# A four-byte tile gets a 64-byte slot, and every tile laid out after it moves by 32 bytes

## The chip, the core and the metric

The kernel is one program on one core of a Trainium2 chip. The metric is the device time of one execution in microseconds. Three executions of the kernel before gave a median of 2630.83 us (2629.59 to 2634.77).

## What is computed

Sixteen sublayers in a row work on one sequence of 256 tokens with 1024 features, all in float32. Cut to what matters here:

```python
# f00 f01 f10 f11: gated feed-forward, width 2816;  g00 g01 g10 g11: the same, width 2752, modulated
h = (silu(gate) * up) @ w_out            # gate, up = x @ w_in
# m0 m1: squared relu, width 4096
h = square(relu(u @ w_ff1)) @ w_ff2
# conv, hgrn (recurrent mixer), dsa, diff, pool, moba: mixers, each ending in
m = o @ w_out                            # o: 256 x 1024, w_out: 1024 x 1024
# pool and moba also attend to a memory
k, v = split(mem_n @ w_mem_kv)
```

Every sublayer is wrapped in an RMS norm and added to `x`.

## The kernel before

The order of the sublayers is f00, conv, f01, f10, hgrn, f11, g00, dsa, g01, g10, diff, g11, pool, m0, moba, m1.

**Weights.** All large weights lie in `wall` as 413 chunks of 1 MB, in the order in which they are used. `_load` (L314) brings a chunk into a `raw` tile (3 buffers). `_split` (L321) makes two float32r tiles of it: ScalarE copies four pieces into `hi` (L330), VectorE subtracts and writes the rest into `lo` (L335); each has 5 buffers. An activation is split the same way into a high and a low tile, and a product is three matmuls: high with high, high with low, low with high.

**Matmuls.** In each, one operand is loaded into the array as a block of 128 x 128 (the profile's PEld, LDWEIGHTS) and the other streams past it (PE, MATMUL). In the profile's `out<-in` the streaming tile is named first and the loaded one second, and the shape behind is that of the streaming operand. Four places matter:

- `u_products` (L545, matmuls at L552 to L554): blocks of `hi` or `lo` are loaded, `xh` or `xl` streams with 256 columns.
- `proj_pair` (L574, L581 to L583): blocks of `xh` or `xl` are loaded, `hi` or `lo` streams with 512 columns. Each sublayer's first products are of this kind, and so is `mem_kv` (L1598), whose loaded tiles are `mh` and `ml`.
- `downs` (L612, L622): a block of the hidden tile is loaded, and `hi` or `lo` streams with 512 columns. In the ten feed-forward blocks the hidden tiles are `hh` and `hl`; in the mixers' output products they are `xh` and `xl`, except in hgrn, where they are `ov` and `oscT` (L1084).
- transposes (L503, L526, L760, L1252, L1331): the tile is loaded, `ident` streams.

The lines of `downs` that pick the operands:

```python
mm = lambda l, r, i, st, sp: nc.tensor.matmul(
    acc[i], lhsT=l[:k, t], rhs=r[:k, 1024 * b + 512 * i:1024 * b + 512 * i + 512], ...)
    yield mm(hh, wh, i, ...)
    yield mm(hh, wl, i, ...)
    yield mm(hl, wh, i, ...)
```

**Where tiles lie.** Pools are stacked in the order in which they are opened (L300 to L307):

```python
self.cst = pool("cst", 1)
self.raw_p = pool("rawp", self.RB)
self.hi_p = pool("hip", self.HB)
self.lo_p = pool("lop", self.HB)
self.act = pool("act", 1)
self.rowp = pool("rowp", 1)
self.tmp = pool("tmp", 1)
self.tiny = pool("tiny", 4)
```

Each sublayer opens its own pools on top of these and closes them at its end. A slot is a whole number of 32-byte steps of each partition. In the built program `hi` begins at byte 54496, 62688, ... of a partition, `lo` at 95456, ..., `xh` at 136416 and `xl` at 144608: all of them 224 bytes past a multiple of 512. The slot of the tile `prime` in `tiny` lies at 172640, and the sublayers' pools begin at 174784, which is 192 past a multiple of 512. `hh` lies at 180928, 182976, ..., `hl` at 189120, ... (207552 and more in m0 and m1), `oscT` at 174784, `ov` at 187072, `mh` at 178880 and `ml` at 187072: all of them at 192.

**The tile that is changed.** `prime` (L432) runs a one-element activation whose result nobody reads, so that ScalarE has the next function's table before it is needed. `finish` (L638) calls it at a sublayer's end, and `conv` once.

Of the kernel before, what the change touches and what calls it, by code (L numbers as in the profile page):

```python
# [11 lines left out]
F32 = mybir.dt.float32  # L12
# [280 lines left out]
class _K:  # L293
# [138 lines left out]
    def prime(self, func, after):  # L432

        n = after.shape[0]
        t = self.tiny.tile([128, 1], F32, name="prime", bufs=1)
        self.nc.scalar.activation(t[:n], after, func, scale=0.0)

    def square(self, src, st, n):
# [1396 lines left out]
```

## Time and profile before

| | |
|---|---|
| median of three executions | 2630.83 us |
| the profiled execution | 2628.67 us |
| its span, from the first to the last instruction | 2626.9 us |
| mean granted TensorE clock | 0.997 |
| HBM read | 550.62 MB, 210 GB/s over the span |

The span is 1.8 us shorter than the time of the same execution. Times inside a profile are microseconds from the span's start. In the profile f00 ends at about 203 us, conv at 336, f01 at 526, f10 at 716, hgrn at 872, f11 at 1063, g00 at 1251, dsa at 1358, g01 at 1546, g10 at 1734, diff at 1856, g11 at 2056, pool at 2125, m0 at 2323, moba at 2440.

### The profile page before, as it was taken

What the parts mean: (1) busy time and instruction counts of PE and PEld (TensorE: products, weight loads), DVE (VectorE), ACT (ScalarE), POOL (GpSimd) and SP (SyncE); (2) the same over time, 40 slices, a digit from 0 to 9 for tenths busy, and PEclk for the clock granted to TensorE, in tenths of its full rate; (3) what the DMA queues carried; (4) which work ended last, traced back from release to release, by engine and by line L of the source; (5) the groups of instructions that cost most, each with busy time, mean ns of one, the idle gap of its engine ahead of it and who ended that gap; (6) DMA issues with size and microseconds to landing.
All of it is one profiled execution on the core that took longest, in us unless ns stands there. A gap on an engine that the chain in (4) does not pass through costs nothing.

```text
span 2626.9 us, 43032 instructions
## 1 busy us (share of the span) xinstructions
PE 2585.0 (98%) x15958; PEld 2286.7 (87%) x15958; DVE 1914.4 (73%) x5151; ACT 1374.9 (52%) x3037; POOL 71.6 (3%) x158
## 2 busy tenths in 40 slices
PE   8999999999999999999999999999999999999999
PEld 7998889989998899899779989977899788977898
DVE  7858587587578875985878778677855866577754
ACT  5545454454545544644664454466644655466543
POOL 0000000000000000000000000000100000000000
PEclk9999999999999999999999999999999999999999
DMA  8847376486425675784548768653555545542552
GB/s 325 305 161 281 145 259 246 150 331 233 169 92 194 258 288 177 279 307 175 177 162 303 264 230 332 219 210 129 210 191 177 187 162 197 187 170 97 192 182 91
DMA packets 92739, 554.53 MB, mean 211 GB/s; under 512 B 10717, under 2 KB 11757, under 8 KB 38385
## 3 DMA queue, kind: packets, MB, share of 16 engines
q1 hardware_dynamic: 92528, 551.79, 57.4%
q8 instruction: 125, 2.05, 0.3%
q14 instruction: 86, 0.70, 0.1%
HBM read 550.62 MB, written 1.13 MB: 210 GB/s over the span
## 4 chain that ended last, share of the span: by engine, by line
PE 58%; issue 34%; DVE 3%; ACT 2%; POOL 1%; DMA 1%; SPq 0%; POOLq 0%; ACTq 0%; DVEq 0%
PE a L622 20%; PE ps L552 8%; PE ps L553 8%; PE ps L554 8%; PE a L581 2%; PE a L583 2%; PE a L582 2%; DVE lo L335 2%; PE a L903 1%; PE tr L503 1%; DMA raw<-in_wall 1%; POOL ry L447 1%; ACT hi L330 1%; ACT junk L441 1%; PE a L1303 0%
## 5 line engine op out<-in xcount | busy, mean ns | idle before, releaser
L335 DVE TENSOR_TENSOR lo<-raw,hi 128x256 fp32r<-128x256 f32 (+1 forms) x2964 | 1158.1, 448 | 387.3 <-ACT hi L330 386.8
L330 ACT ACTIVATE hi<-raw 128x512 fp32r<-128x512 f32 x1652 | 944.3, 623 | 759.2 <-issue 271.3
L552 PE MATMUL ps<-xh,hi 128*128 128x256 f32 x2784 | 789.9, 284 | 0.0
L553 PE MATMUL ps<-xl,hi 128*128 128x256 f32 x2784 | 788.5, 283 | 0.0
L554 PE MATMUL ps<-xh,lo 128*128 128x256 f32 x2784 | 788.2, 283 | 0.0
L553 PEld LDWEIGHTS ps<-xl,hi 128*128 128x128 f32 x2784 | 533.4, 192 | 3.6
L552 PEld LDWEIGHTS ps<-xh,hi 128*128 128x128 f32 x2784 | 533.3, 192 | 3.6
L554 PEld LDWEIGHTS ps<-xh,lo 128*128 128x128 f32 x2784 | 533.4, 192 | 0.1
L622 PE MATMUL a<-hi,hh 128*128 128x512 f32 x960 | 309.6, 396 | 0.0
L622 PE MATMUL a<-lo,hh 128*128 128x512 f32 x960 | 309.3, 396 | 0.0
L622 PE MATMUL a<-hi,hl 128*128 128x512 f32 x960 | 309.3, 396 | 0.0
L622 PEld LDWEIGHTS a<-lo,hh 128*128 128x128 f32 x960 | 179.9, 188 | 43.7
L622 PEld LDWEIGHTS a<-hi,hl 128*128 128x128 f32 x960 | 179.9, 187 | 43.5
L1159 DVE SCALAR_TENSOR_TENSOR adaj<-adaw,cond 128x1024 bf16<-128x1024 f32 x144 | 175.6, 1219 | 42.8 <-DMA adaw<-in_ada 41.6
L622 PEld LDWEIGHTS a<-hi,hh 128*128 128x128 f32 x960 | 174.5, 188 | 36.2 <-ACT hh L697 0.2
L581 PE MATMUL a<-hi,xh 128*128 128x512 f32 x512 | 201.4, 394 | 3.2 <-ACT xh L511 1.8
L583 PE MATMUL a<-hi,xl 128*128 128x512 f32 x512 | 201.9, 396 | 0.6 <-DVE xl L512 0.6
L582 PE MATMUL a<-lo,xh 128*128 128x512 f32 x512 | 200.1, 391 | 0.3 <-DVE lo L335 0.3
L581 PEld LDWEIGHTS a<-hi,xh 128*128 128x128 f32 x512 | 96.6, 189 | 26.5 <-ACT xh L516 5.4
L583 PEld LDWEIGHTS a<-hi,xl 128*128 128x128 f32 x512 | 96.3, 188 | 24.7 <-DVE xl L512 3.2
L582 PEld LDWEIGHTS a<-lo,xh 128*128 128x128 f32 x512 | 96.6, 189 | 20.6 <-DVE lo L335 0.8
L735 ACT ACTIVATE hh<-h 128x256 fp32r<-128x256 f32 x144 | 59.1, 410 | 71.9 <-DVE h L734 71.9
(364 smaller groups left out, 2607.5 us busy)
## 6 DMA issues: line engine op xcount, KB each, us to landing
raw<-in_wall SPq DMA_DIRECT2D x413, 1024.0 KB, 4.8
adaw<-in_ada SPq DMA_DIRECT2D x144, 512.0 KB, 6.8
taps<-in_ctaps SPq DMA_DIRECT2D x10, 1024.0 KB, 7.8
G<-in_rows SPq DMA_DIRECT2D x16, 512.0 KB, 5.7
pg<-in_rows SPq DMA_DIRECT2D x12, 512.0 KB, 4.9
xn<-modd SPq DMA_DIRECT2D x12, 512.0 KB
cond<-condd SPq DMA_DIRECT2D x7, 512.0 KB, 6.1
memt<-in_mem SPq DMA_DIRECT2D x4, 512.0 KB, 3.3
```

What stands on the lines that cost most here:

```text
L330: self.nc.scalar.activation(h[:, c], r[:, c], AF.Copy)
L335: self.nc.vector.tensor_tensor(l[:, c], r[:, c], h[:, c].bitcast(F32), op=OP.subtract)
L441: self.nc.scalar.activation(j, src, AF.Square, scale=1.0 / 32, accum_out=st[:, n:n + 1])
L552: yield self.nc.tensor.matmul(o, lhsT=wh[:, c], rhs=xh[:, k, :], start=(k == 0), stop=False)
L553: yield self.nc.tensor.matmul(o, lhsT=wh[:, c], rhs=xl[:, k, :], start=False, stop=False)
L554: yield self.nc.tensor.matmul(o, lhsT=wl[:, c], rhs=xh[:, k, :], start=False, stop=(k == 7))
L581: yield self.nc.tensor.matmul(p, lhsT=xh[:, k, t], rhs=wh[:, c], start=(k == 0), stop=False)
L582: yield self.nc.tensor.matmul(p, lhsT=xh[:, k, t], rhs=wl[:, c], start=False, stop=False)
L583: yield self.nc.tensor.matmul(p, lhsT=xl[:, k, t], rhs=wh[:, c], start=False, stop=(k == 7))
L622: mm = lambda l, r, i, st, sp: nc.tensor.matmul(acc[i], lhsT=l[:k, t], rhs=r[:k, 1024 * b + 512 * i:1024 * b + 512 * i + 512], start=st, s ...
L735: nc.scalar.activation(hh[:n, b], h[:n], AF.Copy)
L1159: self.nc.vector.scalar_tensor_tensor(junk, self.ada_w.pop(n), 1.0, self.cond, op0=OP.mult, op1=OP.mult, accum_out=self.mods[k][:, c:c + 1])
```

## The change

The tile has 16 elements instead of 1, and its first column is used as before:

```diff
     def prime(self, func, after):
 
         n = after.shape[0]
-        t = self.tiny.tile([128, 1], F32, name="prime", bufs=1)
+
+        t = self.tiny.tile([128, 16], F32, name="prime", bufs=1)[:, :1]
         self.nc.scalar.activation(t[:n], after, func, scale=0.0)
```

Its slot grows from 32 to 64 bytes. The instructions on each engine and their order stay the same. Whatever lies below or before that slot stays: `hi`, `lo`, `xh`, `xl`, `raw`, the rows, `ident`. Whatever comes after it in `tiny`, and every pool of a sublayer, begins 32 bytes later: `hh`, `hl`, `oscT`, `ov`, `mh` and `ml` now lie 224 past a multiple of 512, as the weights do. The mixers' other tiles move by 32 bytes as well, all of one sublayer together.

## Rows read from the trace of the kernel before

**Rows 1.** The page's head and first part: busy time, share, instructions.
```profile
span 2626.9 us, 43032 instructions
...
PE 2585.0 (98%) x15958; PEld 2286.7 (87%) x15958; DVE 1914.4 (73%) x5151; ACT 1374.9 (52%) x3037; POOL 71.6 (3%) x158
```
**Rows 2.** The page's fifth part: output products of the feed-forward blocks (busy us, mean ns).
```profile
L622 PE MATMUL a<-hi,hh 128*128 128x512 f32 x960 | 309.6, 396 | 0.0
L622 PE MATMUL a<-lo,hh 128*128 128x512 f32 x960 | 309.3, 396 | 0.0
L622 PE MATMUL a<-hi,hl 128*128 128x512 f32 x960 | 309.3, 396 | 0.0
```
**Rows 3.** Busy time by engine, most of f01: start:end length, engines, PEclk, DMA share.
```profile
345.00:525.00 180.00, 179.95 (x1205) 165.30 (x1204) 128.38 (x346) 86.68 (x184) 1.72 (x4) 1.00 0.64 228
```
**Rows 4.** Timeline of f01, PE: start us, length us, instruction; 18 rows of two between.
```profile
513.84 0.63 PE L622 MATMUL a<-hi,hh 128*128 128x512 f32 x2
514.31 0.63 PE L622 MATMUL a<-lo,hh 128*128 128x512 f32 x2
...
522.24 0.39 PE L622 MATMUL a<-hi,hh 128*128 128x512 f32 x1
```
**Rows 5.** Timeline of conv's output product, PE; 16 rows of two from first to last.
```profile
315.89 0.62 PE L622 MATMUL a<-hi,xl 128*128 128x512 f32 x2
316.35 0.61 PE L622 MATMUL a<-hi,xh 128*128 128x512 f32 x2
...
323.15 0.39 PE L622 MATMUL a<-hi,xh 128*128 128x512 f32 x1
```
**Rows 6.** Timeline of hgrn's output product, PE; 18 rows of two from first to last.
```profile
860.43 0.63 PE L622 MATMUL a<-hi,ov 128*128 128x512 f32 x2
...
868.83 0.39 PE L622 MATMUL a<-hi,ov 128*128 128x512 f32 x1
```
**Rows 7.** Timeline of moba's memory keys, PE; 25 single matmuls from first to last.
```profile
2316.26 0.40 PE L581 MATMUL ps<-hi,mh 128*128 128x512 f32 x1
...
2322.09 0.39 PE L582 MATMUL ps<-lo,mh 128*128 128x512 f32 x1
```
**Rows 8.** Timeline of the same lines with xh in hgrn; 22 single matmuls.
```profile
842.62 0.39 PE L581 MATMUL ps<-hi,xh 128*128 128x512 f32 x1
...
847.61 0.39 PE L582 MATMUL ps<-lo,xh 128*128 128x512 f32 x1
```
**Rows 9.** Instructions of L622: ns min/median/max of one, first and last start.
```profile
L622 PE MATMUL a<-hi,hh x960: 390/394/497, 48.8 to 2622.3; 128*128 128x512 f32 x192
L622 PE MATMUL a<-lo,hh x960: 392/396/486, 49.2 to 2622.5; 128*128 128x512 f32 x192
...
L622 PE MATMUL a<-hi,xh x160: 387/389/794, 308.6 to 2439.0; 128*128 128x512 f32 x160
...
L622 PE MATMUL a<-hi,ov x32: 393/394/397, 848.1 to 871.8; 128*128 128x512 f32 x32
```
**Rows 10.** VectorE by shape: busy us, mean ns, idle before.
```profile
L335 DVE TENSOR_TENSOR lo<-raw,hi 128x256 fp32r<-128x256 f32 x2624 | 939.4, 417 | 358.1 <-ACT hi L330 357.6
...
L736 DVE TENSOR_TENSOR hl<-h,hh 128x256 fp32r<-128x256 f32 x140 | 58.5, 418 | 1.3 <-ACT hh L735 1.3
```
**Rows 11.** PE by shape, transposes: busy us, mean ns, idle before.
```profile
L503 PE MATMUL tr<-ident,xn 128*128 128x128 f32 x300 | 41.3, 277 | 10.5 <-DVE xn L488 10.4
L1331 PE MATMUL tr<-ident,e 128*128 128x128 f32 x140 | 24.0, 278 | 0.6 <-DVE xl L1277 0.2 <-ACT e L1321 0.2
L1252 PE MATMUL tr<-ident,on 128*128 128x128 f32 x52 | 8.2, 275 | 0.4 <-DVE on L1525 0.4
```
**Rows 12.** Busy time by engine in conv at the lower clock (columns as in Rows 3).
```profile
309.00:314.00 5.00, 5.00 (x13) 3.84 (x13) 3.72 (x8) 4.71 (x10) 0.00 (x0) 0.50 0.00 0
```
**Rows 13.** Timeline of that stretch, PE; four rows of two from first to last.
```profile
309.63 1.05 PE L622 MATMUL a<-lo,xh 128*128 128x512 f32 x2
...
313.05 1.05 PE L622 MATMUL a<-hi,xl 128*128 128x512 f32 x2
```

## The prediction

> **What bounds the kernel now.** I read the page's head first. TensorE's matmuls take 2585.0 of 2626.9 us, VectorE 73% and ScalarE 52% [rows 1], so the question is what sets TensorE's pace. One stage answers it: over 180 us of f01 TensorE is busy for 179.95, VectorE for 128.38 (71%), ScalarE for 86.68 (48%), and the DMA engines for 0.64 of the time [rows 3]. Nothing makes TensorE wait there. A feed-forward block is then as long as its matmuls in a row, and one that starts sooner after its predecessor shortens the block by that much.
>
> The length of a matmul in the profile is not this pace, since matmuls overlap. The pace is the distance between starts, and the timeline gives it. In f01, 18 rows of two matmuls of L622, all on `hh` and `hl`, lie between the starts 513.84 and 522.24: 8.40 us / 36 = 233.3 ns each [rows 4]. In conv's output product, the same line, shape and weights, but with `xh` and `xl` loaded, 16 rows of two lie between 315.89 and 323.15: 7.26 / 32 = 226.9 ns [rows 5]. Both run back to back at the full clock. Why 6.4 ns more?
>
> Three places tell. hgrn's output product loads `ov` and `oscT`, tiles with the shape of `xh` but in a sublayer's own pool: 8.40 / 36 = 233.3 ns [rows 6]. The memory's keys use L581 to L583 with `mh` and `ml`, again of `xh`'s shape: 5.83 / 25 = 233.2 ns [rows 7]. The same lines with `xh` take 4.99 / 22 = 226.8 ns [rows 8]. So neither the line nor the shape nor the way the tile is stepped through sets the pace. What the slow three share is that the loaded tile lies 192 bytes past a multiple of 512 while the streaming `hi` or `lo` lies at 224; in the fast two both lie at 224. The durations say the same: 394 to 396 ns in the median for `hh` and 394 for `ov`, 389 for `xh` [rows 9].
>
> **The change, part by part.** It adds, removes and reorders no instruction. The ten activations that write `prime` still write one element for each partition; their cost is unchanged. What is left is where tiles lie.
>
> *Output products of the feed-forward blocks.* `hh` and `hl` move to 224, so the pair becomes the fast one. There are 3 x 960 = 2880 such matmuls [rows 2] (264 in each of eight blocks, 384 in m0 and m1). 2880 x (233.3 - 226.9) ns = 18.4 us, all of it on the path, since TensorE never pauses there [rows 3].
>
> *hgrn's output.* 96 matmuls on `ov` and `oscT` x 6.4 ns = 0.6 us.
>
> *Memory keys and values*, two sublayers, 96 matmuls on `mh` and `ml`: 96 x (233.2 - 226.8) = 0.6 us. They stand between g11 and pool, and between m0 and moba, back to back with the next products.
>
> *What doesn't change.* The 256-column products stream `xh` past `hi`, neither of which moves. In conv the two float32r tiles that move, `ones` and `bias`, move together, as do the mixers' own float32 pairs.
>
> *Transposes.* Here `ident` stays and the loaded tile moves. The trace has no such tile at its new place, so I bound it by tiles that lie at different places already: `xn` at 224, `e` at 256, 224, 192 and 448, `on` at 256, 224, 192 and 448, which take 277, 278 and 275 ns [rows 11]. A spread of 3 ns over at most some 300 moved transposes is 0.9 us either way; I take zero.
>
> *VectorE and ScalarE* write and read the moved tiles. `lo`, at 224, takes 417 ns for 256 columns, `hl`, at 192, takes 418 [rows 10]: one nanosecond, either way, on engines that are 71% and 48% busy in the block. Zero; the cover is TensorE's own row of matmuls, and without it 144 such instructions would be 0.1 us.
>
> *Sum.* 18.4 + 0.6 + 0.6 = 19.6 us less. The profiled execution took 2628.67 us with a span of 2626.9, so the changed one should take 2609.1 with a span of 2607.3. The median of the three executions lies 2.2 us above the profiled one; **from it I forecast 2611.2 us**.
>
> *Its bounds.* By durations alone [rows 9] a matmul gains 5 to 7 ns: 3072 x 5 = 15 us to 3072 x 7 = 21.5 us. Next late, once the blocks are 1.7 us shorter, is still TensorE: VectorE's 128.38 us in a stretch of 178.3 is 72%.
>
> A rule speaks against all this. The Trainium skill, page "TensorE: Matmul & The Clock Gate", section "Step-by-step: what each phase is for", says that TensorE has two independent read ports into SBUF, one for the streaming operand and one for the weight load, so that loading the next weights takes nothing from the running matmul. By that rule the place of a tile would cost nothing, and the time would stay at 2630.8 us. The trace does not agree with it where the two paces differ for one line and one shape (233.3 against 226.9 ns), though it can't say by itself that the offset is the cause.
>
> **The rivals.**
>
> *No effect.* The pace comes from something else that `hh`, `ov` and `mh` share and `xh` lacks; what remains is that they all lie above byte 174784, `xh` below 152800. A tile that moves by 32 bytes would then gain nothing: 2630.8 us. For it: no row before has a float32r tile in that upper part at offset 224. Against it: within the slow group `hh` and `ov` lie anywhere from 174784 to 211648 and show the same 233.3, and `hi` at 54496 or `lo` at 128224 make no difference either; only the offset in 512 is common to each group. 6%.
>
> *The gain is eaten by the feeding of weights.* The blocks would need 0.9% more bytes in a given time. If chunks then came late half the time, half the gain would stay: 2630.8 - 9.8 = 2621.0 us. For it: the DMA engines are already at 0.64 in f01. Against it: TensorE waits for no weights there, and two chunks stand ready in front of it. 4%.
>
> *Slower, by the clock.* In conv TensorE works at half the clock, 1.2 instead of 2.4 GHz, for a stretch [rows 12]: there the same line takes 3.42 / 8 = 427.5 ns [rows 13], so a stretch of 10 us costs about 5 us. It follows a pause of TensorE in the mixer. If earlier ends of the blocks shifted such pauses so that more of them drew a fall, the loss would have to exceed 19.6 us plus the 5.3 us that 0.2% are: five stretches of 10 us in the six mixers where there is one now. 2630.8 - 19.6 + 5 x 5.1 = 2636.7 us. Against it: the pauses in the mixers are made by their own chains, which the change leaves alone; the mean clock is 0.997. 2%.
>
> **How the numbers follow.** The forecast has 88%. The low end takes the largest gain and the one stretch at half the clock in conv gone, from the fastest of the three executions: 2629.6 - 21.5 - 5 = 2603 us. The high end takes the smallest gain from the slowest of the three: 2634.8 - 15 = 2620 us. This leaves out the rivals (12%) and a little of the forecast's own tails. A measurement can tell about 0.2%, or 5.3 us, from no change. Faster by more: the forecast and the half-eaten gain, 0.92. The same: no effect, 0.06. Slower: 0.02.
>
> **What would show it.** Right: L622 on `hh` and `ov` at a median of about 389 ns, rows of two starting 0.45 instead of 0.47 us apart, `mh` like `xh`; the products of 256 columns, `lo` and the transposes as before; each feed-forward block about 1.7 us shorter, m0 and m1 2.4, the conv, dsa, diff and pool sublayers as long as before; TensorE's busy time near 2565 us. Wrong: `hh` still at 394 to 396 ns (no effect); `hh` at 389 with TensorE waiting for `hi` or `lo` in the blocks (eaten gain); `hh` at 389, the blocks shorter, and the mixers longer at a lower granted clock (slower).

## The result and the profile after

The changed kernel took 2617.28 us in the median of five executions (2615.37 to 2621.91), the kernel before 2633.18 beside it; the ratio is 0.995, with an interval of 0.994 to 0.9961. That is about 16 us faster, where 19.6 were forecast. The profiled execution took 2617.28 us with a span of 2615.5. Code from L435 on stands one line lower in this kernel: L622 is now L623, L581 is L582.

The page's head, part 1 and three groups of part 5 of the kernel after (columns as in [rows 1, 2]):

```profile
span 2615.5 us, 43032 instructions
...
PE 2571.4 (98%) x15958; PEld 2291.9 (88%) x15958; DVE 1913.1 (73%) x5151; ACT 1377.0 (53%) x3037; POOL 69.7 (3%) x158
...
L623 PE MATMUL a<-hi,hh 128*128 128x512 f32 x960 | 305.1, 392 | 0.0
L623 PE MATMUL a<-lo,hh 128*128 128x512 f32 x960 | 304.1, 391 | 0.0
L623 PE MATMUL a<-hi,hl 128*128 128x512 f32 x960 | 303.7, 391 | 0.0
```

TensorE has 13.6 us less of busy time with the same instructions; VectorE and ScalarE are where they were. The durations of L623 show where it is (ns, minimum, median and maximum, as in [rows 9]):

```profile
L623 PE MATMUL a<-hi,hh x960: 388/389/500, 49.7 to 2610.9; 128*128 128x512 f32 x192
L623 PE MATMUL a<-lo,hh x960: 387/389/482, 50.1 to 2611.2; 128*128 128x512 f32 x192
...
L623 PE MATMUL a<-hi,xh x160: 387/390/795, 307.4 to 2429.7; 128*128 128x512 f32 x160
...
L623 PE MATMUL a<-hi,ov x32: 387/389/397, 848.2 to 871.5; 128*128 128x512 f32 x32
```

`hh` and `ov` are at 389 ns, as `xh` already was. The timeline of PE in f01 (start, length) gives the pace of the stretch that [rows 4] showed, between fourteen rows of two:

```profile
512.83 0.61 PE L623 MATMUL a<-lo,hh 128*128 128x512 f32 x2
513.28 0.62 PE L623 MATMUL a<-hi,hl 128*128 128x512 f32 x2
...
519.18 0.39 PE L623 MATMUL a<-hi,hh 128*128 128x512 f32 x1
```

6.35 us / 28 = 226.8 ns from start to start. The memory's keys in the timeline, 33 single matmuls (before: [rows 7]):

```profile
2305.80 0.39 PE L582 MATMUL ps<-hi,mh 128*128 128x512 f32 x1
...
2313.05 0.39 PE L584 MATMUL ps<-hi,ml 128*128 128x512 f32 x1
```

7.25 / 32 = 226.6 ns, against 233.2. TensorE is still what bounds a block; the window of f01 (columns as in [rows 3]):

```profile
345.00:525.00 180.00, 179.91 (x1208) 166.43 (x1207) 129.81 (x348) 87.92 (x187) 2.58 (x6) 1.00 0.64 233
```

**By sublayer.** I cut each trace where a sublayer's first product starts (f00 where its transposes start). The ten feed-forward blocks together take 1901.0 us, 14.5 less than before (1915.5). In this count the memories' keys and values belong to the blocks that they follow, g11 and m0; each of the two went from 11.2 to 10.9 us, so that the blocks' own products gave 13.9 us. The single block f01 went from 190.1 to 188.3, f10 from 190.4 to 189.1, m1 from 187.2 to 185.1. The six mixers together take 706.9, 3.0 more (703.9). Nearly all of that is hgrn, 156.2 to 160.2. Its waits in the kernel after (who waited for whom, us, times, longest):

```profile
DVE masks L1050 <- DMA xn<-in_k_masks: 6.1, 1, 6.1
...
ACT hi L330 <- DVE lo L335: 3.4, 1, 3.4
...
PE tr L690 <- ACT junk L688: 2.8, 1, 2.8
```

In the kernel before, these three were:

```profile
DVE masks L1049 <- DMA xn<-in_k_masks: 3.9, 1, 3.9
...
ACT hi L330 <- DVE lo L335: 1.2, 1, 1.2
...
PE tr L689 <- ACT junk L687: 0.6, 1, 0.6
```

VectorE waited 2.2 us longer for a table of constants, ScalarE stood behind VectorE, and TensorE behind ScalarE. After that pause TensorE worked at half the clock (1.2 GHz) for 3.4 us, as the window shows (columns as in [rows 3]):

```profile
739.90:743.30 3.40, 3.40 (x18) 3.40 (x17) 1.96 (x5) 3.39 (x8) 0.00 (x0) 0.50 0.77 313
```

Is that the change's doing? The first experiment asks it.

### The profile page after: what moved, and what is told of

Its sections match the earlier page's. It is cut to its first block, busy times and chain, and to the rows that moved or that the text cites. A ratio compares the mean times of both kernels' runs of the same rounds, so it can differ in the third digit from the quotient of the medians.

```text
span 2615.5 us, 43032 instructions
## 1 busy us (share of the span) xinstructions
PE 2571.4 (98%) x15958; PEld 2291.9 (88%) x15958; DVE 1913.1 (73%) x5151; ACT 1377.0 (53%) x3037; POOL 69.7 (3%) x158
## 4 chain that ended last, share of the span: by engine, by line
PE 57%; issue 35%; DVE 3%; ACT 2%; POOL 1%; DMA 1%; SPq 0%; POOLq 0%; ACTq 0%; DVEq 0%
PE a L623 19%; PE ps L554 8%; PE ps L555 8%; PE ps L553 8%; PE a L582 2%; PE a L584 2%; PE a L583 2%; PE a L904 1%; DVE lo L335 1%; PE tr L504 1%; ACT hi L330 1%; DMA raw<-in_wall 1%; ACT junk L442 1%; POOL ry L448 1%; PE a L1304 0%
## 5 line engine op out<-in xcount | busy, mean ns | idle before, releaser
L553 PE MATMUL ps<-xh,hi 128*128 128x256 f32 x2784 | 791.1, 284 | 0.0
L554 PE MATMUL ps<-xl,hi 128*128 128x256 f32 x2784 | 790.4, 284 | 0.0
L555 PE MATMUL ps<-xh,lo 128*128 128x256 f32 x2784 | 790.2, 284 | 0.0
L553 PEld LDWEIGHTS ps<-xh,hi 128*128 128x128 f32 x2784 | 535.2, 192 | 3.1
L554 PEld LDWEIGHTS ps<-xl,hi 128*128 128x128 f32 x2784 | 535.2, 192 | 3.0
L555 PEld LDWEIGHTS ps<-xh,lo 128*128 128x128 f32 x2784 | 535.2, 192 | 0.1
L623 PE MATMUL a<-hi,hh 128*128 128x512 f32 x960 | 305.1, 392 | 0.0
L623 PE MATMUL a<-lo,hh 128*128 128x512 f32 x960 | 304.1, 391 | 0.0
L623 PE MATMUL a<-hi,hl 128*128 128x512 f32 x960 | 303.7, 391 | 0.0
L623 PEld LDWEIGHTS a<-lo,hh 128*128 128x128 f32 x960 | 180.3, 188 | 38.1
L623 PEld LDWEIGHTS a<-hi,hl 128*128 128x128 f32 x960 | 180.3, 188 | 37.6
L582 PE MATMUL a<-hi,xh 128*128 128x512 f32 x512 | 202.1, 395 | 3.7 <-ACT xh L512 1.8
L623 PEld LDWEIGHTS a<-hi,hh 128*128 128x128 f32 x960 | 175.2, 189 | 31.3 <-ACT hh L698 0.2
L582 PEld LDWEIGHTS a<-hi,xh 128*128 128x128 f32 x512 | 97.1, 190 | 26.8 <-ACT xh L517 5.4
```

The costliest lines, as they stand in the source:

```text
L553: yield self.nc.tensor.matmul(o, lhsT=wh[:, c], rhs=xh[:, k, :], start=(k == 0), stop=False)
L554: yield self.nc.tensor.matmul(o, lhsT=wh[:, c], rhs=xl[:, k, :], start=False, stop=False)
L555: yield self.nc.tensor.matmul(o, lhsT=wl[:, c], rhs=xh[:, k, :], start=False, stop=(k == 7))
L582: yield self.nc.tensor.matmul(p, lhsT=xh[:, k, t], rhs=wh[:, c], start=(k == 0), stop=False)
L623: mm = lambda l, r, i, st, sp: nc.tensor.matmul(acc[i], lhsT=l[:k, t], rhs=r[:k, 1024 * b + 512 * i:1024 * b + 512 * i + 512], start=st, s ...
```

## The experiments

The ratios are to the kernel before, run beside each. "Pace" is, over all matmuls of a kind in the profiled execution, the mean distance to the start of the next matmul, without gaps (over 150 ns for 256 columns, 260 for 512). For L622 on `hh` and `hl` it went from 233.2 to 227.6 ns with the change.

**The changed kernel again** (no edit).

> The changed kernel once more, to see how much of the missing 4 us is chance. If hgrn's 4 us came from the moved tiles, hgrn takes about 160 us again and its masks land 2 us late again; if from one execution's transfers and clock, hgrn is back near 156 us and the time falls towards 2613 us. L623 on hh keeps a median of 389 ns either way.

2613.94 us (2611.06 to 2615.12), ratio 0.9933 [0.9921, 0.9946]. The profiled execution has a span of 2609.3. Its ten blocks take 1901.0 us, the same as in the first profile of this kernel; its mixers take 700.6 instead of 706.9, with hgrn at 156.1. The same window of hgrn:

```profile
739.90:743.30 3.40, 3.36 (x29) 3.01 (x27) 3.09 (x8) 3.40 (x10) 0.00 (x0) 1.00 0.19 77
```

Full clock, and VectorE waited 3.9 us for the masks, as before. So hgrn's 4 us come and go from one execution to the next. From here on the blocks' sum is my measure of the change, and the whole time only where a ratio has an interval.

**One half of the change each.** Blocks alone: `prime` as before, and in the feed-forward pools

```diff
+            pad = hp.tile([128, 8], F32, name="pad", bufs=1)
+            nc.gpsimd.memset(pad[:, :1], 0.0)
```

> The old prime tile, and a pad of 32 bytes at the bottom of the feed-forward blocks' own pools: hh and hl lie at 224, all mixers' tiles where they were. Theory (the offset sets the pace): hh at 389 ns, ov and mh still at 394 to 396, 16 to 18 us less than before. Rival (the moved mixer tiles took 4 us back): hgrn at 156 us and a time about 3 us below that of the changed kernel.

2617.25 us, ratio 0.9948 [0.9936, 0.9961]; blocks 1902.4. In its profile hgrn takes 160.9 us with every tile of the mixers where it was, so a long hgrn needs no moved tile. The others alone: the changed kernel with the same `pad` of 120 elements, which puts `hh` and `hl` back to 192 in 512:

> The new prime tile, and a pad in the blocks' pools that puts hh and hl back at 192: only ov, oscT, mh, ml and the mixers' other tiles move. Theory: hh at 394 to 396 ns, ov and mh at 389, 1.2 us less than before, which is within what a measurement can tell. Rival (moving the mixers' tiles costs): 2 to 4 us more than before, all of it in hgrn.

2629.26 us, ratio 0.9986 [0.9978, 0.9995]; blocks 1915.2, near the 1915.5 before. The feed-forward blocks carry most of the gain; the rest, hgrn's output and the memories, is worth some 1 to 6 us by this interval, 1.2 by the pace.

**The masks earlier.** In hgrn, into a tile of their own, at the sublayer's start:

```diff
+            mi = hp.tile([128, 512], I32, name="mi", bufs=1)
+            nc.sync.dma_start(mi[:, :448], self.a["k_masks"])
...
-            mi = self.tmp.tile([128, D], I32, name="xn", bufs=1)
-            nc.sync.dma_start(mi[:, :448], self.a["k_masks"])
```

> The changed kernel, with hgrn's masks brought in at hgrn's start into a tile of their own of 2048 bytes (no other offset in 512 changes), so that VectorE no longer waits for them. If the late masks cost hgrn its time, hgrn falls by 2 to 6 us against the changed kernel of the same call (VectorE waited 3.9 us for them before and 6.1 after); if the wait is covered, nothing changes.

2612.46 us, ratio 0.9931 [0.9918, 0.9945]: not to be told from the unchanged repeat beside it. The wait is gone from hgrn, whose length is 156.1 us as in the repeat. It costs nothing in an ordinary execution; that it made the 4 us in the first profile is argued from the chain of waits, not shown.

**Other offsets for the loaded tile.** `prime` with 24, 32, 48 and 80 elements; the first reads

```diff
-        t = self.tiny.tile([128, 16], F32, name="prime", bufs=1)[:, :1]
+        t = self.tiny.tile([128, 24], F32, name="prime", bufs=1)[:, :1]
```

and puts `hh`, `ov` and `mh` at 256 in 512 (the others at 288, 352, 480); `hi` and `lo` stay at 224.

> The prime tile has 96 bytes: hh, ov and mh lie at 256, 32 past the weights' 224 instead of 32 short of it. Theory (equal offsets are what counts): the slow pace, hh at 394 to 396 ns, ov and mh too, a time like that of the kernel before. Rival (192 alone is bad, any other place is good): hh at 389 and a time near 2612 us.

> The prime tile has 128 bytes: hh, ov and mh lie at 288, which leaves the same rest by 64 as 224 but not by 128 or 512. If only the rest by 64 counts, hh takes 389 ns and the time is near 2612 us; if the whole 512 count, 394 to 396 ns and the time of the kernel before.

> The tile prime takes 192 bytes, so that hh, hl, ov, oscT, mh and ml lie at 352 in 512, 128 bytes past the place of hi and lo (224). If the remainder by 256 decides (equal at a distance of 256, unequal at 32 and 64, as the runs so far have it), L623 on hh, ov and mh is as slow as before: 394 to 396 ns in the median, starts 233 ns apart, and the time near that of the kernel before, 2629 to 2635 us. If the remainder by 128 decides, 388 to 389 ns and 227 ns apart, and 2611 to 2622 us. If the distance counts in size, some third pace.

> The prime tile has 320 bytes: hh, ov and mh lie at 480, half of 512 past the weights' 224, the same rest by 128 and by 256. If the rest by 256 or less counts, hh takes 389 ns; if the whole 512 count, 394 to 396 ns, and if it is the distance that counts, this is the farthest and the slowest of all.

L622 in the four, by the durations (256, 288, 352 and 480 in this order):

```profile
L622 PE MATMUL a<-hi,hh x960: 389/396/497, 50.5 to 2628.4; 128*128 128x512 f32 x192
```
```profile
L622 PE MATMUL a<-hi,hh x960: 391/394/501, 48.9 to 2622.5; 128*128 128x512 f32 x192
```
```profile
L622 PE MATMUL a<-hi,hh x960: 387/395/504, 48.9 to 2618.8; 128*128 128x512 f32 x192
```
```profile
L622 PE MATMUL a<-hi,hh x960: 387/389/499, 49.6 to 2615.8; 128*128 128x512 f32 x192
```

Blocks: 1916.3, 1916.7, 1913.6 and 1902.0 us. Quick again at 480, which is 256 away from 224: the remainder by 256 counts, not by 512 as I had put it. At 128 away the pace is 232.3 ns, little better than unequal by 32 or 64 (233.1, 233.4). The single whole times were 2634.76, 2628.84, 2625.14 and 2622.14 us.

**All at another place.** 32 bytes more in the lowest pool, so that everything above moves and `hi`, `lo`, `xh`, `hh` and `mh` all lie at 256:

```diff
+        self.pad = c.tile([128, 8], F32, name="pad")
+        nc.gpsimd.memset(self.pad, 0.0)
         self.x = c.tile([128, 2, D], F32, name="x")
```

> The changed kernel with 32 more bytes at the bottom, so that hi, lo, xh, xl and hh, ov, mh all lie at 256. Theory (equal offsets): hh at 389 ns, xh at 389, time as that of the changed kernel, 2611 to 2617 us. Rival (224 itself is the good place): all of them at 394 to 396, and since all 512-column products are then slow, about 6 ns x 5000 = 30 us more than the changed kernel.

2616.2 us in one run; `hh` at 389 ns in the median, blocks 1901.4. So 224 is nothing special; what counts is the distance between the two tiles.

**`xh` moved, `hi` not.** `prime` as before, and a pad of 32 bytes ahead of `xh`: `xh` and `xl` at 256, and what lies above them up to `prime` 32 bytes further too; `hi`, `lo`, `hh` and `mh` are where the changed kernel has them.

```diff
+            pad = self.act.tile([128, 8], F32, name="pad")
+            nc.gpsimd.memset(pad, 0.0)
             self.the_act = (self.act.tile([128, 8, 256], F32R, name="xh"), ...
```

> Tile prime takes 32 bytes again, and 32 bytes of padding stand ahead of xh in its pool (written once by GpSimd): hi and lo lie at 224 in 512, xh and xl at 256, hh, hl, ov and mh at 224. If unequal remainders cost wherever one operand is loaded and the other streams, the products on xh slow down too: those of 512 columns with xh or xl loaded (1536 of L582 to L584 in the first products, 480 in the mixers, 480 of L623, 96 more) by 6 ns each, 2592 x 6 = 16 us, and the 8352 products of 256 columns with hi or lo loaded and xh or xl streaming from 119.6 to 122 to 126 ns each, 20 to 53 us: 2650 to 2685 us. If only 512 streaming columns are sensitive: 227 to 233 ns on those and 119.6 ns on the others, 2628 to 2634 us. If it was the place above byte 174784 that made hh slow, not the offset: no product changes, 2611 to 2622 us.

None of the three. 2603.86 us in one run, quicker than the changed kernel; blocks 1879.7. The 512-column products on `xh` did slow down as expected (233.2 ns instead of 227.6). But the 8352 products of 256 columns got quicker, 116.7 ns instead of 119.9. Their durations (L555 here is L552 of before), and L553 of the changed kernel for comparison:

```profile
L555 PE MATMUL ps<-xh,hi x2784: 276/280/468, 37.4 to 2576.1; 128*128 128x256 f32 x199
```
```profile
L553 PE MATMUL ps<-xh,hi x2784: 277/283/468, 37.3 to 2589.5; 128*128 128x256 f32 x199
```

Equal remainders are the quick case for 512 streaming columns and a slow one for 256. I had put the 256-column products at "neither moves" and never asked whether their equal offsets were good.

**The turn earlier.** Is the missing part of the gain a wait for the next sublayer's `xl`? In `finish` the first half's turn is issued 14 or 18 matmuls before the end instead of 10:

```diff
-            at, turn = (n - self.BEHIND, lambda: self.split_t(0, src, act)) if src else (None, None)
+            at, turn = (n - 14, lambda: self.split_t(0, src, act)) if src else (None, None)
```

> The changed kernel, but with the turn of the first half of the tokens (transposes, xh, xl for the next sublayer) issued 14 instead of 10 matmuls before the end of a sublayer's output products, 0.9 us earlier. If the next sublayer's first products wait for xl because the output products now end sooner, PE's waits for xl of L513 at the starts of sublayers fall from 0.25 to 0.5 us each to near none, and the time is 2 to 6 us shorter than the changed kernel's: 2608 to 2612 us against 2613 to 2617. If the tile xn is not ready that early, the transposes wait in PE's queue ahead of the last 14 matmuls, and the time is the same or longer. If these waits are no part of what was missing from the forecast, no change.

> As with 14, but 18 matmuls before the end. If the wait for xl is what counts and xn is ready: as short as with 14, no shorter. If xn is late: PE waits in each sublayer at the transposes for VectorE's xn, 0.5 to 1 us in each of up to 15 sublayers, 8 to 15 us longer than the changed kernel: 2621 to 2632 us.

2615.55 us, ratio 0.9941 [0.9925, 0.9958], and 2615.98, ratio 0.9937 [0.9923, 0.9951]: by the whole time neither differs from the changed kernel. The waits of the weight loads on the first half's `xl` (the line that L513 is now, L512 before), in before, after and with 14:

```profile
PEld a L583 <- DVE xl L512: 3.2, 8, 0.7
```
```profile
PEld a L584 <- DVE xl L513: 4.3, 8, 0.7
```
```profile
PEld a L584 <- DVE xl L513: 2.6, 3, 1.1
```

And the blocks: 1898.4 us with 14, 2.6 less than the changed kernel, and 1901.3 with 18, where the transposes wait for `xn` instead (L504's weight loads 13.5 us in all, 11.6 in the changed kernel). The blocks' first products, summed from start to next start, show the same: 226.5 us before, 228.8 after (228.1 in the repeat), 226.4 with 14. So some 2 us of the gain did go into the starts of sublayers. A gain of 2.6 us is below what the mixers' scatter lets the whole time show.

**Both shapes at their quick place.** The changed kernel, but `hi` and `lo` of a chunk share a tile with 256 bytes to spare, and the chunks of `u_products` are written some bytes further in it; here 8 elements, 32 bytes. All other chunks stay at 224 in 256, like `xh`, `hh` and `mh` (what lies above the chunks moves up by 1280 bytes, five times 256).

```diff
-        h = self.hi_p.tile([128, 2048], F32R, name="hi")
-        l = self.lo_p.tile([128, 2048], F32R, name="lo")
+        at = 8 if self.plan[i][0] == "U" else 0
+        w = self.hi_p.tile([128, 4160], F32R, name="w")
+        h, l = w[:, at:at + 2048], w[:, at + 2048:at + 4096]
```

> The changed kernel, but hi and lo of a chunk share one tile with 256 bytes to spare, and the chunks of u_products (256 streaming columns, hi or lo loaded) are written 32 bytes further in their slot: their hi and lo lie at 0 in 256, xh and xl at 224; all other chunks, xh, hh, ov and mh stay at 224. If the pace depends on the pair of remainders and on the shape, with 256 columns quicker on unequal remainders (116.5 ns in the run with xh moved) and 512 columns quicker on equal ones (227 ns), both are had: 8352 x 3.1 ns = 26 us less than the changed kernel's 2614 to 2617, so 2588 to 2591 us, ratio to before near 0.983, with the products of 512 columns at 389 ns in the median. If what counted there was that xh lay at 256 (the moved streaming tile itself, wherever the loaded one is), 119.6 ns stay and the time is 2611 to 2622 us. If the pace follows the sign of the distance (the loaded tile 32 bytes below the streaming one there, 32 above here), the products of 256 columns get slower than 119.6 ns: 2622 us and more.

> As u32, with the chunks of u_products 64 bytes further. If any unequal remainder does it: 116 to 117 ns, and within 5 us of u32. If the distance counts in size: another pace, and a time that follows it by 8.4 us for each ns.

> As u32, with the chunks of u_products 128 bytes further, half the period of 256. For 512 columns a distance of 128 was slow in part (231.5 ns, between 227 and 233.3). If the two shapes mirror each other, 256 columns gain in part: about 118 ns, some 12 us slower than u32. If any unequal remainder does it: 116 to 117 ns.

> As u32, with the chunks of u_products 192 bytes further, 64 below in 256. If only the size of the distance counts, u64's 117.5 to 118 ns, some 8 us slower than u224. If the side counts beside it: a pace below u64's, 116 to 117 ns, and a time near u224's.

> As u32, with the chunks of u_products 224 bytes further, which is 32 below in 256: the same sign of the distance as in the run with xh moved. If the sign counts, 116.5 ns here and a slower u32; if only inequality counts, the two are within 5 us.

> u224 unchanged, timed in rounds. By its one run: 2586 to 2594 us, ratio to before 0.983 to 0.986, with the 256-column products at 116.7 ns and those of 512 columns at 227. If that one run was a chance, the pace of u32 (118.3 ns) and 2604 to 2609 us come back.

What came out, by where the loaded `hi` or `lo` lies from the streaming `xh` (mod 256):

| loaded tile from streaming tile | pace, 256 columns | ten blocks | time |
|---|---|---|---|
| 0 (the change, its repeat) | 119.9 ns | 1901.0 us | 2617.28, 2613.94 us |
| 32 above | 118.3 | 1889.7 | 2607.11, ratio 0.9904 [0.9887, 0.9921] |
| 64 above | 117.7 | 1883.9 | 2598.61, one run |
| 128 | 119.9 | 1902.4 | 2622.49, one run |
| 64 below | 117.7 | 1884.6 | 2601.79, one run |
| 32 below | 116.7 | 1874.8 | 2591.95, ratio 0.985 [0.9836, 0.9863] |

The 512-column products kept their 227 to 228 ns in all six rows. So the pair's distance sets the pace, not the moved tile as such: 32 below gives 116.7 ns whether `xh` or the chunk was moved. That `hi` and `lo` now share a tile doesn't do it either, since 116.7 came without that and 119.9 with it. The side counts at 32 bytes (116.7 against 118.3), not at 64. u32's forecast of 2588 us missed because I had carried over the pace of the run with `xh` moved, in which `hi` lies 32 below `xh`, to a tile 32 above. The last row is that same distance: one run had given 2589.33 us with blocks of 1876.1, and 2586.78 to 2595.13 us in five executions held it. The forecast for 128 (about 118 ns if the two shapes mirror each other) missed as well. Its timeline in f01, 30 starts after the first:

```profile
400.00 0.28 PE L556 MATMUL ps<-xh,w 128*128 128x256 f32 x1
...
403.50 0.28 PE L556 MATMUL ps<-xh,w 128*128 128x256 f32 x1
```

3.50 us / 30 = 116.7 ns. The changed kernel in the same place, 30 starts again:

```profile
400.02 0.28 PE L553 MATMUL ps<-xh,hi 128*128 128x256 f32 x1
...
403.62 0.28 PE L553 MATMUL ps<-xh,hi 128*128 128x256 f32 x1
```

3.60 / 30 = 120.0 ns. The quickest version takes TensorE's busy time down to

```profile
PE 2544.9 (98%) x15958; PEld 2262.1 (87%) x15958; DVE 1920.5 (74%) x5151; ACT 1375.8 (53%) x3037; POOL 70.0 (3%) x158
```

and is 38 us quicker than the kernel before (2629.94 beside it), 22 to 25 us quicker than the change.

## Where the prediction held, and which step of it failed

**What bounds the kernel** held: the gain is TensorE's pace, and within the blocks nothing else got in its way. At their starts something did, as said below.

**The cause, offsets of loaded and streaming tile,** held for the products that the prediction costed, and was shown: `hh` slow at 192, 256, 288 and 352, quick at 224 and 480, with nothing changed but where the tiles above `prime` lie. The rival of no effect (a place above byte 174784) is out, and so is the half-eaten gain: TensorE is busy for 179.91 of 180 us in f01. That a tile's place costs nothing, as the prediction derived it from the Trainium skill's two independent read ports ("TensorE: Matmul & The Clock Gate", "Step-by-step: what each phase is for"), is out too: the same instructions took 389 or 394 to 396 ns in the median by the place of the loaded tile alone. What the ports do in the slow case no run shows.

**The remainder by 512** was the wrong period: 256, by the run at 480. It did not touch the forecast.

**The sum, 19.6 us, is the step that failed, in its first term.** "2880 x (233.3 - 226.9) ns = 18.4 us, all of it on the path": the blocks' own products gave 13.9 us. The term was too large for two reasons.

*The pace.* 226.9 ns came from 32 matmuls of conv, an undisturbed stretch [rows 5]. Over all these matmuls the two paces are 233.2 before and 227.6 after, so 2880 x 5.6 = 16.1 us. (`xh` in the same line had 228.0 over the whole kernel before; that mean, not the best stretch, was the number to take.) What the best stretch left out shows in any row of output products. Of one row of 24 in f01, here are the lines that begin with the first, the seventh and the matmul behind the last; before:

```profile
445.28 0.62 PE L622 MATMUL a<-hi,hh 128*128 128x512 f32 x2
...
446.67 0.63 PE L622 MATMUL a<-hi,hh 128*128 128x512 f32 x2
...
450.87 0.28 PE L552 MATMUL ps<-xh,hi 128*128 128x256 f32 x1
```

and the same row after:

```profile
442.98 0.63 PE L623 MATMUL a<-hi,hh 128*128 128x512 f32 x2
...
444.37 0.62 PE L623 MATMUL a<-hi,hh 128*128 128x512 f32 x2
...
448.45 0.28 PE L553 MATMUL ps<-xh,hi 128*128 128x256 f32 x1
```

The first six take 1.39 us / 6 = 231.7 ns each in both kernels; the other 18 go from 4.20 / 18 = 233.3 to 4.08 / 18 = 226.7. Over all rows of the ten blocks the first five starts behind other products or a pause go from 232.6 to 232.0 ns, and those after them from 233.4 to 226.7. So the head of each row gains next to nothing; why it does not, no run shows.

*The path.* "Next late ... is still TensorE" failed in part: 13.9 us came, not 16.1. The output products end sooner, and the next sublayer's first products wait longer for `xl`; in the blocks they take 2.3 us more than before (1.6 in the repeat). The runs with an earlier turn bear this out: with 14 matmuls the first products are back at 226.4 us, and the waits at L513 fall from 4.3 to 2.6 us.

hgrn's output and the memories gave 93 matmuls at 233.3 to 227.6 and 96 at 233.2 to 226.7, about 0.5 and 0.6 us, as forecast.

**The mixers "as long as before"** held in the mean of two profiles and not in the profile of the result: 703.9 before, 706.9 in the first profile after, 700.6 in the second of the same kernel. hgrn alone moved by 4 us between two executions of one kernel. I took the blocks' gain from a profile and the time from a median as if the mixers added nothing to either.

Against this the times read plainly: 14.5 us in the blocks, the memories among them, and 0.5 in hgrn's output make 15 us. The two series of the changed kernel gave 15.9 and 18.5 us (2633.18 - 2617.28 and 2632.4 - 2613.94), a scatter that the mixers' 6 us covers.

**The clock rival** had the right place and not the force: in the first profile after there are two more stretches at half clock than before, both in mixers (hgrn and diff), and the next execution had neither. Beside conv's stretch the kernel before has a shorter one in dsa, from 1277.3 us (granted clock 0.50), which the prediction left out.

**256-column products at zero** was right for this change, since none of their tiles moved. It hid the larger gain: 8352 x (119.9 - 116.7) = 26.7 us, against the 16 of the change.

## What to carry to other kernels

Where matmuls run back to back, compare the start-to-start pace of one line on different tiles; when two paces differ for the same shape, list the byte offsets of loaded and streaming tile and try them by padding, for each shape by itself, since the good distance for one was a bad one for another. Take the pace from all matmuls of a kind, not from the cleanest stretch. And judge a change of half a per cent by the part of the program it touches: the rest of this one differed by 6 us between two profiles of the same kernel (mixers 706.9 and 700.6 us).

## What was not expected

- The pace of a float32r matmul depends on the distance of its loaded from its streaming tile modulo 256 bytes: with 512 columns 227.6 ns at equal places, 233.2 at 32 below, 233.1 at 32 above, 233.4 at 64 above, 232.3 at 128; with 256 columns 119.9, 116.7, 118.3, 117.7 and 119.9 ns. What inside the chip makes it so stays open: the runs show where, not why. Other distances, and other shapes, were not tried.
- At 128 bytes the three 256-column products no longer share one pace: the durations in the median were 281 ns at L554, 284 at L555 and 285 at L556 of that kernel, where the other distances keep the three within 2 ns.
- The same program's sublayers with pauses in TensorE's work differ by several us from one execution to the next (hgrn 160.2 and 156.1 in the changed kernel, diff 121.0 and 126.5 in the quickest one), the longer one each time with a stretch at half the clock. The feed-forward blocks' sum repeated to 0.1 us in the first of these pairs (1901.0 and 1901.0) and to 1.3 in the second (1876.1 and 1874.8).
